# A hybrid decoder layer on one core: the decay tile in quarters, two longer waits, gate chunks moved to other buffers

## The chip, the core and the metric

The kernel runs on one core of one Trainium2 chip. The metric is device time in microseconds (us) of one execution, input in device memory to output in device memory. TensorE (PE) does matmuls, VectorE (DVE) and ScalarE (ACT) elementwise work, GpSimd (POOL) elementwise work and some transfers, SyncE (SP) only issues transfers. Each engine runs its instructions in the order in which the program lists them for it; it waits for another engine or for a transfer by semaphore, and everything behind a waiting instruction on that engine waits too.

## What is computed

One layer over a sequence of 1024 positions, model width 2048, float32, cut to what matters here:

```python
xn   = rms_norm(h, norm_w)
proj = xn @ w_in                                  # 2048 x 7184
qkv, z_a, b_raw, a_raw, u_b, v_b, z_b = split(proj)
q, k, v = split(silu(causal_conv4(qkv)))          # 8 heads x 128, q and k l2-normalised
beta = sigmoid(b_raw)
g    = -exp(a_log) * softplus(a_raw + dt_bias)    # log decay per head and position
gc   = cumsum(g)                                  # inside chunks of 64
decay = where(incl, exp(where(incl, gc[i] - gc[j], 0)), 0)
L    = where(strict, (k*beta) @ k.T * decay, 0)   # (I + L) solved per chunk
attn = where(incl, q @ k.T * decay, 0)
# state recurrence over chunks -> o_a ; o_a = rms_norm(o_a) * silu(z_a)
s    = chunked_causal_spatial(layer_norm(v_b))    # 128x128 matrix per group
o_b  = u_b * s * silu(z_b)
out  = rms_norm(h + concat(o_a, o_b) @ w_out)
```

## The kernel before

The sequence is done in two halves of 512 positions, one after the other (names end in 0 or 1 for the half: `em0`, `wl1_17_3`). A float32 product is done as three matmuls: each operand is split into a rounded part (`h`) and the rest (`l`), and PE does x_h w_h, x_l w_h and x_h w_l (L235, L236, L238). The splits of the weights are made on the spot: SP loads a raw chunk (`wr`, L184), ACT rounds it (`wh`, L134), DVE subtracts (`wl`, L135). A projection of 128 output columns has 48 matmuls in four chunks (`wl0_17_0` to `wl0_17_3` are the four chunks of column block 17 in half 0).

**Order.** `run` (L210) walks through the chunks, with the loads of the next ones started ahead. Work that belongs to a finished projection (convolution, gates, the solve of a pair of heads, output of a pair) is written as generators: `yield n` hands back for n ticks, and `tick` is called after every six matmuls or so of a projection. A scheduler then fixes each engine's order at build time. So a `yield` says how many matmuls stand between two steps in PE's order, and what stands between them in the order of the other engines follows.

**First tiles** (`first_tiles`, L259). Each half starts with one chunk loop over 16 blocks of the model width, which makes the first key and query projections (`wrf`, `whf`, `wlf`; banks 0 and 1) and, in four more PSUM banks, the 16 gate columns together with 256 columns of the spatial value (`V0` = 272 columns). The latter's chunks (`wrv0`, then `whv`, `wlv`) are called gate chunks below: eight of them, [128, 2, 272], in the same weight buffers as all others (tags `wr`, `wh`, `wl`), which are therefore 2176 bytes per partition long.

**Buffers of 8 KB** (pool `big`, tag `b8`, four of them). They hold, at various times, the keys and queries of a pair (`kq`), the spatial values (`vn`), the decay tile (`em`), a solve buffer (`fs`), and in the output phase the four blocks of output rows (`h`, stored at L829).

**Decay tile** (`task_gates`, L378 to L389). The cumulative log decay is written to device memory and read back broadcast into `em`, a tile of [128, 32 x 64]. Four times in a row: POOL subtracts (L386), DVE takes the minimum with a mask (L387), ACT takes the exponential (L388). `task_q` of each head waits until the whole tile is entered (L488), multiplies its own 4 x 64 columns on POOL (L491), and makes the products `gl` (L502) and `gae` (L509) on DVE.

**Pairs** (`task_pair`, L535). Inside the solve, PE fills `yp` (L572), ACT copies it negated to `ys` (L576), `yield 1`, and PE multiplies again (L581). At the end of a pair POOL scales the output `o` (L649), a transposed copy goes through device memory (`swap`, L410: DVE L415, POOL's transfers L420 and L423), and after `yield W_SWO` (L654, 16 ticks) DVE makes the gated result from the reloaded `ut` (L660), which SP stores.

**Spatial groups** (L728 to L737): PE fills `sp` (L732), DVE reads it into `s` (L734), POOL scales (L737). `s` shares two buffers (`ut`) with the reloaded tiles of the last pair, and `sp` shares two PSUM banks (tag `gen`) with other small products.

Of the kernel before, what the change touches and what calls it, by code (L numbers as in the profile page):

```python
# [8 lines left out]
F32 = mybir.dt.float32  # L9
F32R = mybir.dt.float32r  # L10
# [7 lines left out]
P = 128  # L18
# [5 lines left out]
NT = T // P  # L24
# [7 lines left out]
def kernel(ctx, tc, x_tok, x_t, w_in, w_v0, w_vb, w_out, conv_w, norm_w, a_log, dt_bias,  # L32
# [5 lines left out]
    wp = pool("wp", bufs=4)  # L38
    big = pool("big", bufs=4)
# [11 lines left out]
    def bc(ap, shape):  # L51
        return ap.broadcast_to(shape)
# [126 lines left out]
        nc.scalar.copy(rb, rp)  # L179
        return rb  # L180

    def w_chunk(src, shape, name, keep=None):
        raw = wp.tile(shape, F32, tag="wr", bufs=3, name=f"wr{name}")
        nc.sync.dma_start(raw, src)  # L184
        hi, lo = keep or (wp.tile(shape, F32R, tag="wh", name=f"wh{name}"), wp.tile(shape, F32R, tag="wl", name=f"wl{name}"))
        split(hi, lo, raw)
        return hi, lo
# [38 lines left out]
    V0 = 256 + 2 * H  # L226
# [32 lines left out]
    def first_tiles(hf, xs, env, done):  # L259


        accs, sqs = [], []
        for q in range(KT // 2):
            def prep(q=q):
                ks = slice(2 * q, 2 * q + 2)
                raw = wp.tile([P, 2, 2, P], F32, tag="wr", bufs=3, name=f"wrf{hf}_{q}")
                hi = wp.tile([P, 2, 2, P], F32R, tag="wh", name=f"whf{hf}_{q}")
                lo = wp.tile([P, 2, 2, P], F32R, tag="wl", name=f"wlf{hf}_{q}")
                sqs_, sqs[:] = list(sqs), []
                for i in range(2):  # L270
                    x, sq = x_load(hf, 2 * q + i)
                    xs.append(x)
                    sqs.append(sq)
                    nc.sync.dma_start(raw[:, i], w_in[(H, 0)[i], :, ks, :])
                    split(hi[:, i], lo[:, i], raw[:, i])
                vb = w_chunk(w_v0[q], [P, 2, V0], f"v0{hf}_{q}")
                for sq in sqs_ + (sqs if q == KT // 2 - 1 else []):
                    sq()
                if hf == 0 and q == 5:
                    conv_constants()  # L280
                return hi, lo, vb
# [32 lines left out]
    def task_gates(hf, accs, env, gt):  # L314
# [65 lines left out]
        em = big.tile([P, H * NT, 64], F32, tag="b8", name=f"em{hf}")  # L380
        for c in range(2):
            nc.gpsimd.dma_start(em[c * 64:(c + 1) * 64], gcd[c].partition_broadcast(64))
        yield 3
        for q in range(4):
            e4 = em[:, q * 8:(q + 1) * 8, :]
            nc.gpsimd.tensor_tensor(e4, e4, bc(gc[:, q * 8:(q + 1) * 8].unsqueeze(2), [P, 8, 64]), op=ALU.subtract)  # L386
            nc.vector.tensor_tensor(e4, e4, bc(cap.unsqueeze(1), [P, 8, 64]), op=ALU.min)  # L387
            nc.scalar.activation(e4, e4, AF.Exp)  # L388
        gt.update(em=em)  # L389


    def scaled(acc, rb, name):
# [39 lines left out]
        return s4  # L432


    W_SWO = 16
    W_SO0 = 4
    W_CONV = 7
    W_SWAP = 7
# [5 lines left out]
    W_DMA2 = 18  # L444
    W_GATES = 12
    W_LN = 12

    def task_k(hf, h, st, pr, acc):
        gt, hh = st["gt"], h % 2
# [29 lines left out]
    def task_q(hf, h, st, pr, acc):  # L479
        gt, hh = st["gt"], h % 2  # L480
        hd = pr["hd"][hh]
# [3 lines left out]
        yield W_SW0  # L485
        z = swap(y, kq[:, 1, :], y, f"q{hf}_{h}", nc.sync)
        yield W_CONV + (W_FIRST if h == 0 else 0)
        while "em" not in gt or "kd" not in hd:  # L488
            yield 1
        em = gt["em"][:, h * NT:(h + 1) * NT, :]  # L490
        nc.gpsimd.tensor_tensor(em, em, bc(hd["c"].unsqueeze(2), [P, NT, 64]), op=ALU.mult)  # L491

        wq = wk.tile([P, NT, 4, 64], F32, tag="wq", bufs=2, name=f"wq{hf}_{h}")
# [18 lines left out]
        if hh == 1:  # L512
            spawn(task_pair(hf, h // 2, st, pr))
# [23 lines left out]
    def task_pair(hf, p, st, pr):  # L537
        gt, heads = st["gt"], pr["hd"]
# [35 lines left out]
        for c in range(2):  # L574
            b = c * 64 + 32
            nc.scalar.activation(ys[b:b + 32], yp[b:b + 32], AF.Copy, scale=-1.0)  # L576
        yield 1
        for c in range(2):
            a, b = c * 64, c * 64 + 32
            for u in range(2 * NT):  # L580
# [52 lines left out]
        for h2, hd in enumerate(heads):  # L633
# [19 lines left out]
            yield 1  # L653
        yield W_SWO  # L654
        while not all("z" in hd for hd in heads):
# [298 lines left out]
```

## Time and profile before

| | us |
|---|---|
| median of 3 runs | 1827.82 (1825.97 to 1830.06) |
| the profiled execution, own time | 1829.9 |
| its span, first to last instruction | 1828.2 |
| PE busy | 1794.5 (98%) |
| DVE busy | 1149.2 (63%) |
| ACT busy | 733.1 (40%) |
| POOL busy | 263.0 (14%) |

The mean granted TensorE clock of the profiled execution is 0.992 of full speed. In a timeline row, the first column is the start, counted from the first instruction, the second the time from the start of the first to the end of the last of the instructions put together in the row; the count stands behind the x, and brackets give how long the engine had been idle before, with what released it. Matmuls overlap: one of 512 columns takes 0.4 us from start to end, but starts follow each other at 0.23 to 0.24 us. In the windows, PEclk is the mean granted TensorE clock of the stretch.

### The profile page before, as it was taken

Reading aid. Unit: us, or ns where it says so; the run is one execution under the profiler, and the core shown is the slowest. Engines: PE = TensorE matmul, PEld = TensorE weight load, DVE = VectorE, ACT = ScalarE, POOL = GpSimd, SP = SyncE. Lnnn points to the kernel's source line nnn. Section 1 sums busy time; section 2 is a strip of 40 time slices with the busy share of each in tenths; the row PEclk is TensorE's granted clock in tenths of the full one; section 3 lists DMA queues with packets and bytes.
Section 4 is the critical chain, followed back from the end, with each engine's and each line's share of the span. In section 5 each row is a group of like instructions: output and inputs, shape, how many; then the busy total and the mean of one; then the engine's idle time right before and its main releaser. Section 6 shows DMA issues by size and latency. Waiting matters only on the chain.

```text
span 1828.2 us, 27404 instructions
## 1 busy us (share of the span) xinstructions
PE 1794.5 (98%) x9526; PEld 1496.2 (82%) x9526; DVE 1149.2 (63%) x2797; ACT 733.1 (40%) x1656; POOL 263.0 (14%) x318
## 2 busy tenths in 40 slices
PE   9989999999999999999999899999999999999997
PEld 8878788888997888888888687887889978888886
DVE  7788697987646334433657887969785553344343
ACT  6543535445242222322636445354442422233232
POOL 3120130301202000011302101212021030000110
PEclk9999999999999999999999999999999999999999
DMA  7545354464424334733455453544544243355443
GB/s 223 134 130 139 90 143 123 112 164 117 134 81 138 103 103 129 219 121 116 132 194 145 119 139 96 155 107 123 140 122 129 78 122 101 100 158 158 123 140 132
DMA packets 164410, 239.16 MB, mean 131 GB/s; under 512 B 35472, under 2 KB 64176, under 8 KB 164016
## 3 DMA queue, kind: packets, MB, share of 16 engines
q1 hardware_dynamic: 154656, 215.35, 41.5%
q0 software_dynamic: 4864, 13.67, 3.0%
q10 hardware_dynamic: 4752, 8.40, 1.5%
q8 instruction: 74, 1.21, 0.3%
q14 instruction: 64, 0.52, 0.1%
HBM read 200.61 MB, written 36.73 MB: 130 GB/s over the span
## 4 chain that ended last, share of the span: by engine, by line
PE 88%; DVE 4%; DMA 4%; ACT 2%; issue 1%; SPq 0%; POOL 0%; ACTq 0%; POOLq 0%; DVEq 0%
PE acc L235 17%; PE acc L238 16%; PE acc L236 16%; PE vb L775 7%; PE oa L884 6%; PE oa L883 6%; PE oa L885 6%; PE ds L620 2%; PE p L609 1%; DMA wr<-w_in 1%; DVE cv L403 1%; PE ga L500 1%; PE up L594 1%; PE wp L599 1%; PE sp L732 1%
## 5 line engine op out<-in xcount | busy, mean ns | idle before, releaser
L235 PE MATMUL acc<-xh,wh 128*128 128x512 f32 x1472 | 599.3, 407 | 2.5 <-ACT wh L134 2.5
L238 PE MATMUL acc<-xh,wl 128*128 128x512 f32 x1472 | 584.7, 397 | 9.1 <-DVE wl L135 9.0
L236 PE MATMUL acc<-xl,wh 128*128 128x512 f32 x1472 | 580.7, 395 | 0.0
L134 ACT CAST wh<-wr 128x512 fp32r<-128x512 f32 x368 | 226.8, 618 | 493.6 <-PE acc L236 413.9
L135 DVE TENSOR_TENSOR wl<-wr,wh 128x512 fp32r<-128x512 f32 x368 | 255.6, 696 | 178.9 <-ACT wh L134 177.4
L238 PEld LDWEIGHTS acc<-xh,wl 128*128 128x128 f32 x1472 | 279.0, 190 | 75.2 <-DVE wl L135 10.7
L235 PEld LDWEIGHTS acc<-xh,wh 128*128 128x128 f32 x1472 | 278.7, 189 | 62.2 <-issue 3.5
L236 PEld LDWEIGHTS acc<-xl,wh 128*128 128x128 f32 x1472 | 279.3, 190 | 57.7 <-issue 0.7
L885 PE MATMUL oa<-who,ml 128*128 128x512 f32 x472 | 185.3, 393 | 0.0
L884 PE MATMUL oa<-wlo,mh 128*128 128x512 f32 x472 | 185.1, 392 | 0.0
L883 PE MATMUL oa<-who,mh 128*128 128x512 f32 x472 | 185.1, 392 | 0.0
L135 DVE TENSOR_TENSOR wlo<-wro,who 128x512 fp32r<-128x512 f32 x118 | 89.0, 756 | 145.6 <-ACT who L134 145.5
L134 ACT CAST who<-wro 128x512 fp32r<-128x512 f32 x118 | 72.7, 617 | 149.4 <-PE oa L885 140.1
L775 PE MATMUL vb<-whvb,xh 128*128 128x256 f32 x384 | 110.7, 288 | 0.0
L403 DVE SCALAR_TENSOR_TENSOR cv<-pc,cw,cv 128x511 f32<-128x511 f32 (+1 forms) x144 | 107.8, 749 | 4.6 <-ACT cv L400 2.6
L775 PE MATMUL vb<-whvb,xl 128*128 128x256 f32 x384 | 108.4, 282 | 0.0
L775 PE MATMUL vb<-wlvb,xh 128*128 128x256 f32 x384 | 108.3, 282 | 0.0
L884 PEld LDWEIGHTS oa<-wlo,mh 128*128 128x128 f32 x472 | 88.6, 188 | 20.3
L883 PEld LDWEIGHTS oa<-who,mh 128*128 128x128 f32 x472 | 88.6, 188 | 20.1
L885 PEld LDWEIGHTS oa<-who,ml 128*128 128x128 f32 x472 | 88.5, 188 | 20.0
L556 DVE TENSOR_TENSOR fs<-fs,fst 32x31 f32<-32x31 f32 (+15 forms) x248 | 88.5, 357 | 4.1
L554 DVE TENSOR_TENSOR fst<-fs 32x31 f32<-32x31 f32 (+15 forms) x248 | 87.3, 352 | 4.1
(239 smaller groups left out, 2366.4 us busy)
## 6 DMA issues: line engine op xcount, KB each, us to landing
wr<-w_in SPq DMA_DIRECT2D x368, 256.0 KB, 3.1
wro<-w_out SPq DMA_DIRECT2D x128, 256.0 KB, 2.7
wrvb<-w_vb SPq DMA_DIRECT2D x48, 256.0 KB, 2.7
xr<-x_t SPq DMA_DIRECT2D x32, 256.0 KB, 3.9
mr<-mix_d ACTq DMA_DIRECT2D x32, 256.0 KB, 3.4
xres<-x_tok SPq DMA_DIRECT2D x32, 256.0 KB, 3.5
out<-h SPq DMA_DIRECT2D x14, 512.0 KB, 2.8
wrv<-w_v SPq DMA_DIRECT2D x16, 272.0 KB, 2.8
```

The source lines that it names most:

```text
L134: nc.scalar.copy(hi, src)
L135: nc.vector.tensor_tensor(lo, src, hi.bitcast(F32), op=ALU.subtract)
L235: nc.tensor.matmul(acc, hi[:, kk, :], xh, start=(k == 0), stop=False)
L236: nc.tensor.matmul(acc, hi[:, kk, :], xl, start=False, stop=(last and lo is None))
L238: nc.tensor.matmul(acc, lo[:, kk, :], xh, start=False, stop=last)
L403: nc.vector.scalar_tensor_tensor(cv[:, s:], acc[:, :T - s], w, cv[:, s:], op0=ALU.mult, op1=ALU.add)
L554: nc.vector.tensor_tensor(tv, bc(lu[:, k, k + 1:].unsqueeze(2), [32, n, m]), bc(xu[:, k:k + 1, 0:m], [32, n, m]), op=ALU.mult)
L556: nc.vector.tensor_tensor(xu[:, k + 1:, 0:m], xu[:, k + 1:, 0:m], tv, op=ALU.subtract)
L775: nc.tensor.matmul(a, l[:, tsl], r[:, k % 2, :], start=fl, stop=sp_, skip_group_check=True)
L883: nc.tensor.matmul(acc[t], mh[:, tsl], hi[:, 0, :], start=(k == 0), stop=False)
L884: nc.tensor.matmul(acc[t], mh[:, tsl], lo[:, 0, :], start=False, stop=False)
L885: nc.tensor.matmul(acc[t], ml[:, tsl], hi[:, 0, :], start=False, stop=(k == k1))
```

## The change

Four things are changed. The gate chunks no longer use the weight buffers: the raw data of three chunks go into one 8 KB buffer (`v0r`), and each chunk's rounded part and rest together into another (`v0`), from the pool with tag `b8`. The weight buffers are then all 2048 bytes per partition. The decay tile is entered quarter by quarter: each quarter (two heads) is subtracted on POOL, then after two ticks minimum and exponential follow, and `task_q` of a head waits for its own quarter only; the wait before the first quarter is 5 ticks in place of 3. `W_SWO` is 20 in place of 16. The wait between the two `yp` products is 3 ticks in place of 1.

```diff
--- before.py
+++ after.py
@@ -179,8 +179,9 @@
         nc.scalar.copy(rb, rp)
         return rb
 
-    def w_chunk(src, shape, name, keep=None):
-        raw = wp.tile(shape, F32, tag="wr", bufs=3, name=f"wr{name}")
+    def w_chunk(src, shape, name, keep=None, raw=None):
+        if raw is None:
+            raw = wp.tile(shape, F32, tag="wr", bufs=3, name=f"wr{name}")
         nc.sync.dma_start(raw, src)
         hi, lo = keep or (wp.tile(shape, F32R, tag="wh", name=f"wh{name}"), wp.tile(shape, F32R, tag="wl", name=f"wl{name}"))
         split(hi, lo, raw)
@@ -259,7 +260,7 @@
     def first_tiles(hf, xs, env, done):
 
 
-        accs, sqs = [], []
+        accs, sqs, vraw = [], [], []
         for q in range(KT // 2):
             def prep(q=q):
                 ks = slice(2 * q, 2 * q + 2)
@@ -273,7 +274,10 @@
                     sqs.append(sq)
                     nc.sync.dma_start(raw[:, i], w_in[(H, 0)[i], :, ks, :])
                     split(hi[:, i], lo[:, i], raw[:, i])
-                vb = w_chunk(w_v0[q], [P, 2, V0], f"v0{hf}_{q}")
+                if q % 3 == 0:
+                    vraw.append(big.tile([P, 3, 2, 288], F32, tag="b8", name=f"v0r{hf}_{q}"))
+                v2 = big.tile([P, 2, 2, 288], F32R, tag="b8", name=f"v0{hf}_{q}")[:, :, :, 0:V0]
+                vb = w_chunk(w_v0[q], None, None, (v2[:, 0], v2[:, 1]), vraw[-1][:, q % 3, :, 0:V0])
                 for sq in sqs_ + (sqs if q == KT // 2 - 1 else []):
                     sq()
                 if hf == 0 and q == 5:
@@ -380,13 +384,16 @@
         em = big.tile([P, H * NT, 64], F32, tag="b8", name=f"em{hf}")
         for c in range(2):
             nc.gpsimd.dma_start(em[c * 64:(c + 1) * 64], gcd[c].partition_broadcast(64))
-        yield 3
+        yield W_EM
+
+        gt["em"] = []
         for q in range(4):
             e4 = em[:, q * 8:(q + 1) * 8, :]
             nc.gpsimd.tensor_tensor(e4, e4, bc(gc[:, q * 8:(q + 1) * 8].unsqueeze(2), [P, 8, 64]), op=ALU.subtract)
+            yield 2
             nc.vector.tensor_tensor(e4, e4, bc(cap.unsqueeze(1), [P, 8, 64]), op=ALU.min)
             nc.scalar.activation(e4, e4, AF.Exp)
-        gt.update(em=em)
+            gt["em"].append(e4)
 
 
     def scaled(acc, rb, name):
@@ -432,7 +439,7 @@
         return s4
 
 
-    W_SWO = 16
+    W_SWO = 20
     W_SO0 = 4
     W_CONV = 7
     W_SWAP = 7
@@ -444,6 +451,7 @@
     W_DMA2 = 18
     W_GATES = 12
     W_LN = 12
+    W_EM = 5
 
     def task_k(hf, h, st, pr, acc):
         gt, hh = st["gt"], h % 2
@@ -485,9 +493,9 @@
         yield W_SW0
         z = swap(y, kq[:, 1, :], y, f"q{hf}_{h}", nc.sync)
         yield W_CONV + (W_FIRST if h == 0 else 0)
-        while "em" not in gt or "kd" not in hd:
-            yield 1
-        em = gt["em"][:, h * NT:(h + 1) * NT, :]
+        while len(gt.get("em", ())) <= h // 2 or "kd" not in hd:
+            yield 1
+        em = gt["em"][h // 2][:, hh * NT:(hh + 1) * NT, :]
         nc.gpsimd.tensor_tensor(em, em, bc(hd["c"].unsqueeze(2), [P, NT, 64]), op=ALU.mult)
 
         wq = wk.tile([P, NT, 4, 64], F32, tag="wq", bufs=2, name=f"wq{hf}_{h}")
@@ -574,7 +582,7 @@
         for c in range(2):
             b = c * 64 + 32
             nc.scalar.activation(ys[b:b + 32], yp[b:b + 32], AF.Copy, scale=-1.0)
-        yield 1
+        yield 3
         for c in range(2):
             a, b = c * 64, c * 64 + 32
             for u in range(2 * NT):
```

The lines behind the change are eight higher in the new file at the places below (L387 is L394, L502 is L510; L135 stays).

DVE in half 0, from the minimum on the decay tile to the products of head 0, before. `em0` is the decay tile, `wl0_17_0` the rest of the first weight chunk of column block 17, `gl0_0` and `gae0_0` head 0's products:

```order
L130 SCALAR_TENSOR_TENSOR ce0_1_1098<-rst_k0_1_1100,ce0_1_1098 128x4
L387 TENSOR_TENSOR em0_972<-em0_972,cap_96 128x512 x4
L467 TENSOR_TENSOR nk0_1_1096<-ce0_1_1098,ssk0_1_1090 128x4
L468 TENSOR_TENSOR cc0_1_1097<-ce0_1_1098 128x4
L135 TENSOR_TENSOR wl0_17_0_1124<-wr0_17_0_1121,wh0_17_0_1123 128x512
L502 TENSOR_TENSOR gl0_0_1070<-ga0_0_1061,em0_972 128x256
L509 TENSOR_TENSOR gae0_0_1073<-ga0_0_1061,em0_972 64x4x64 x2
```

and now, from the first minimum on:

```order
L394 TENSOR_TENSOR em0_959<-em0_959,cap_96 128x512
L484 TENSOR_TENSOR kd0_1_1068<-pc0_9_864,ce0_1_1048 128x512
L135 TENSOR_TENSOR wl0_17_0_1074<-wr0_17_0_1071,wh0_17_0_1073 128x512
L422 STREAM_TRANSPOSE pc0_1_1011<-kq0_0_756 128x4x4x32
L135 TENSOR_TENSOR wl0_17_1_1105<-wr0_17_1_1102,wh0_17_1_1104 128x512
L394 TENSOR_TENSOR em0_959<-em0_959,cap_96 128x512
L510 TENSOR_TENSOR gl0_0_1123<-ga0_0_1114,em0_959 128x256
L517 TENSOR_TENSOR gae0_0_1126<-ga0_0_1114,em0_959 64x4x64 x2
L135 TENSOR_TENSOR wl0_17_2_1149<-wr0_17_2_1146,wh0_17_2_1148 128x512
L401 TENSOR_TENSOR pc0_16_1164<-acc0_16_1026,rb0_713 128x512
L394 TENSOR_TENSOR em0_959<-em0_959,cap_96 128x512
L415 COPY tails_126<-pc0_16_1164 128x3
```

The four minima stood together ahead of `wl0_17_0`. Now one stands ahead of it, together with head 1's scaled key `kd0_1`, and the other three stand between the chunks that follow.

DVE in half 1, the rows up to the rest of the last chunk of column block 17 (`wl1_17_3`), before; the four minima and `gl1_0` stand further ahead:

```order
L469 TENSOR_TENSOR cc1_1_9788<-cc1_1_9788,g1_beta_9419 128x4
L405 SCALAR_TENSOR_TENSOR cv1_16_9875<-tails_126,cw_99,cv1_16_9875 128x2
L470 TENSOR_TENSOR ce1_1_9789<-cc1_1_9788,g1_ekd_9622 128x4
L403 SCALAR_TENSOR_TENSOR cv1_16_9875<-pc1_16_9873,cw_99,cv1_16_9875 128x509
L476 TENSOR_TENSOR kd1_1_9809<-pc1_9_9564,ce1_1_9789 128x512
L405 SCALAR_TENSOR_TENSOR cv1_16_9875<-tails_126,cw_99,cv1_16_9875 128x3
L135 TENSOR_TENSOR wl1_17_3_9887<-wr1_17_3_9884,wh1_17_3_9886 128x512
```

and now (`cv1_16` is the convolution of column block 16, `pc1_16` its input):

```order
L484 TENSOR_TENSOR kd1_1_9746<-pc1_9_9538,ce1_1_9726 128x512
L394 TENSOR_TENSOR em1_9635<-em1_9635,cap_96 128x512
L410 SCALAR_TENSOR_TENSOR cv1_16_9844<-pc1_16_9842,cw_99,cv1_16_9844 128x511
L412 SCALAR_TENSOR_TENSOR cv1_16_9844<-tails_126,cw_99,cv1_16_9844 128x1
L410 SCALAR_TENSOR_TENSOR cv1_16_9844<-pc1_16_9842,cw_99,cv1_16_9844 128x510
L510 TENSOR_TENSOR gl1_0_9801<-ga1_0_9792,em1_9635 128x256
L517 TENSOR_TENSOR gae1_0_9804<-ga1_0_9792,em1_9635 64x4x64 x2
L412 SCALAR_TENSOR_TENSOR cv1_16_9844<-tails_126,cw_99,cv1_16_9844 128x2
L410 SCALAR_TENSOR_TENSOR cv1_16_9844<-pc1_16_9842,cw_99,cv1_16_9844 128x509
L412 SCALAR_TENSOR_TENSOR cv1_16_9844<-tails_126,cw_99,cv1_16_9844 128x3
L394 TENSOR_TENSOR em1_9635<-em1_9635,cap_96 128x512
L135 TENSOR_TENSOR wl1_17_3_9859<-wr1_17_3_9856,wh1_17_3_9858 128x512
```

Here `wl1_17_3` still stands behind the convolution, head 0's products and three of the four minima; the fourth is behind it. `kd1_1` has moved in front of the convolution.

PE at the start of half 1, rows of the first block, before (`first1_0` and `first1_1` are the key and query banks, `first1_2` to `first1_5` those of the gate chunks):

```order
L294 MATMUL first1_1_8891<-xh1_0_8714,whf1_0_8710 128x512
L295 MATMUL first1_1_8891<-xl1_0_8715,whf1_0_8710 128x512
L296 MATMUL first1_1_8891<-xh1_0_8714,wlf1_0_8711 128x512
L299 MATMUL first1_2_8892<-whv01_0_8732,xh1_0_8714 128x272
L300 MATMUL first1_2_8892<-wlv01_0_8733,xh1_0_8714 128x272
L301 MATMUL first1_2_8892<-whv01_0_8732,xl1_0_8715 128x272
```

and now, where the first gate chunk (`v01_0`) is used:

```order
L300 MATMUL first1_1_8872<-xh1_10_9038,wlf1_5_9035 128x512
L298 MATMUL first1_0_8871<-xh1_11_9047,whf1_5_9034 128x512
L299 MATMUL first1_0_8871<-xl1_11_9048,whf1_5_9034 128x512
L300 MATMUL first1_0_8871<-xh1_11_9047,wlf1_5_9035 128x512
L298 MATMUL first1_1_8872<-xh1_11_9047,whf1_5_9034 128x512
L303 MATMUL first1_2_8873<-v01_0_8718,xh1_0_8701 128x272
L303 MATMUL first1_3_8874<-v01_0_8718,xh1_0_8701 128x272
L303 MATMUL first1_4_8875<-v01_0_8718,xh1_0_8701 128x272
```

The first use of a gate chunk was the seventh matmul of the half. It is now the 71st, behind those of blocks 0 to 10 and most of block 11 for key and query; the matmuls of the gate chunks follow after that. On SP, the first three gate loads of half 1 now stand behind the stores of the first two blocks of output rows of half 0, the next three behind those of all four.

## Rows read from the trace of the kernel before

**Rows 1.** The page: busy time, share of the span and instructions of each engine

```profile
PE 1794.5 (98%) x9526; PEld 1496.2 (82%) x9526; DVE 1149.2 (63%) x2797; ACT 733.1 (40%) x1656; POOL 263.0 (14%) x318
```

**Rows 2.** Timeline of PE: start, us, engine, line, tiles [idle before <-releaser]

```profile
97.25 0.80 PE L238 MATMUL acc<-xh,wl 128*128 128x512 f32 x1 [5.92 <-DVE wl L135]
...
186.74 1.07 PE L581 MATMUL yp<-tt,ys 32*32 32x32 f32 x32 [1.74 <-ACT ys L576]
...
579.54 1.47 PE L732 MATMUL sp<-wmt,vn 128*128 128x128 f32 x8 [2.06 <-DVE s L734]
...
1009.61 0.50 PE L235 MATMUL acc<-xh,wh 128*128 128x512 f32 x1 [2.48 <-ACT wh L134]
...
1013.45 0.79 PE L238 MATMUL acc<-xh,wl 128*128 128x512 f32 x1 [3.11 <-DVE wl L135]
...
1201.19 0.97 PE L581 MATMUL yp<-tt,ys 32*32 32x32 f32 x28 [0.87 <-ACT ys L576]
...
1485.15 0.80 PE L732 MATMUL sp<-wmt,vn 128*128 128x128 f32 x2 [2.74 <-DVE s L734]
```

**Rows 3.** Windows: start:end, length, busy of each engine, PEclk, DMA share, GB/s

```profile
96.00:102.00 6.00, 4.75 (x11) 3.79 (x12) 5.92 (x15) 2.51 (x5) 1.11 (x2) 0.50 0.44 109
188.00:192.00 4.00, 4.00 (x17) 3.42 (x18) 2.75 (x14) 0.75 (x2) 0.00 (x0) 0.61 0.46 112
580.00:584.00 4.00, 4.00 (x16) 3.34 (x15) 3.42 (x4) 0.00 (x0) 1.80 (x3) 0.57 0.53 179
1013.00:1018.00 5.00, 4.55 (x12) 3.62 (x13) 3.95 (x9) 2.05 (x4) 0.00 (x0) 0.59 0.63 165
1199.00:1207.00 8.00, 7.13 (x66) 5.80 (x65) 5.06 (x19) 3.97 (x13) 1.04 (x1) 1.00 0.37 90
```

**Rows 4.** Timeline of DVE, half 0, at the decay tile

```profile
90.60 5.42 DVE L387 TENSOR_TENSOR em<-em,cap 128x512 f32<-128x512 f32 x4 [2.44 <-POOL em L386]
...
96.51 0.68 DVE L135 TENSOR_TENSOR wl<-wr,wh 128x512 fp32r<-128x512 f32 x1
```

**Rows 5.** Timeline of POOL, the decay subtracts of both halves

```profile
89.52 4.94 POOL L386 TENSOR_TENSOR em<-em,gs 128x512 f32<-128x512 f32 x4 [4.80 <-DMA em<-gcd]
...
998.29 4.58 POOL L386 TENSOR_TENSOR em<-em,gs 128x512 f32<-128x512 f32 x4 [2.25 <-DMA em<-gcd]
```

**Rows 6.** Timeline of DVE, half 1, at the decay tile

```profile
999.28 0.69 DVE L135 TENSOR_TENSOR wl<-wr,wh 128x512 fp32r<-128x512 f32 x1 [3.79 <-ACT wh L134]
...
999.89 1.01 DVE L465 TENSOR_SCALAR ssk<-ssk 128x4 f32<-128x4 f32 x1
...
1004.70 2.49 DVE L387 TENSOR_TENSOR em<-em,cap 128x512 f32<-128x512 f32 x4
...
1008.43 0.42 DVE L502 TENSOR_TENSOR gl<-ga,em 128x256 f32<-128x256 f32 x1 [0.51 <-POOL em L491]
...
1012.71 1.28 DVE L135 TENSOR_TENSOR wl<-wr,wh 128x512 fp32r<-128x512 f32 x2
```

**Rows 7.** Timeline of POOL, half 0, last pair, transfers of the two heads

```profile
564.50 2.99 POOL L420 DMA_DIRECT2D swapo<-ut  x4 [1.04 <-DVE ut L415]
...
573.62 0.57 POOL L423 DMA_DIRECT2D ut<-swapo  x1
```

**Rows 8.** Timeline of DVE, half 0, last pair

```profile
577.94 0.75 DVE L660 SCALAR_TENSOR_TENSOR o<-ut,hnw,z 128x512 f32<-128x512 f32 x1 [2.55 <-DMA ut<-swapo]
```

**Rows 9.** Timeline of PE, first matmuls of half 1

```profile
912.81 0.40 PE L294 MATMUL first<-xh,whf 128*128 128x512 f32 x1
913.05 0.40 PE L295 MATMUL first<-xl,whf 128*128 128x512 f32 x1
```

**Rows 10.** Timeline of SP, the output stores of half 0

```profile
920.30 9.15 SPq L829 DMA_DIRECT2D out<-h  x8
```

**Rows 11.** The page, DMA issues: out<-in, engine, count, KB each, us to landing

```profile
out<-h SPq DMA_DIRECT2D x14, 512.0 KB, 2.8
```

**Rows 12.** Timeline of DVE, last normalisation of an output row block

```profile
927.66 0.74 DVE L824 SCALAR_TENSOR_TENSOR h<-h,sth,fw 128x512 f32<-128x512 f32 x1
```

## The prediction

> **What bounds the kernel now.** I read the page's table of busy times first. PE is busy 1794.5 us [rows 1] of a span of 1828.2 us, the profiled execution's own time being 1829.9 us. So no matmul goes away and at most some 33 us can be won: the places where PE stands, and the slow clock after them. Then I went through PE's timeline for idle time in brackets. Seven stalls matter [rows 2]: 5.92 us in half 0 and 2.48 and 3.11 us in half 1 where a weight split is late (released by DVE's `wl` or ACT's `wh`), 1.74 and 0.87 us before the second `yp` product (released by ACT's copy `ys`), 2.06 and 2.74 us before a spatial product (released by DVE's `s`). Sum: 18.92 us. The rest of PE's idle time is in gaps of under half a microsecond, the first microsecond and the output chain behind the last matmul; the change does not touch these.
>
> The third view is the windows behind the stalls. There the granted clock is near the lower of its two levels (1.2 of 2.4 GHz) [rows 3], and what that costs is the busy time multiplied by what is missing from 1: 4.75 x 0.50 = 2.4 us after the 5.92-us stall, 4.00 x 0.39 = 1.6 after the 1.74, 4.00 x 0.43 = 1.7 after the 2.06, 4.55 x 0.41 = 1.9 after the two of half 1; for the 2.74 I put 1.7 as an estimate from the 2.06. After the 0.87 the clock is 1.00: that one costs only itself. Together 9.3 us. All that the change can take away at these seven places is therefore 28.2 us.
>
> **Decay tile, half 0.** PE wanted `wl0_17_0` at 97.25 - 5.92 = 91.33 us [rows 2]. On DVE it stood behind four minima of 5.42 us in all, which began at 90.60 when POOL's first quarter was there, and two small instructions; it ran from 96.51 for 0.68 us [rows 4]. Now one minimum and `kd0_1` stand ahead of it. The four minima lay beside POOL's four subtracts (4.94 us from 89.52 [rows 5]) and took 5.42 / 4 = 1.36 us each; the four of half 1, after POOL had finished at 1002.87, took 2.49 / 4 = 0.62 [rows 5, 6]. So I take 1.36 for the one minimum, and 0.68 (the row of `wl`) for `kd0_1` and `wl0_17_0` each: 90.60 + 1.36 + 0.68 + 0.68 = 93.3. The stall is then 2.0 us, with 1.7 us of slow clock behind it, as after the 2.06: 3.7 in place of 8.3, a gain of 4.6 us. If nothing is slowed by POOL, the split ends at 92.6, the stall is 1.3, and the clock may hold as it did after 0.87: a gain of 7.0. If all three are slowed to 1.36, it ends at 94.7: stall 3.3 and 1.9 of clock, a gain of 3.1. The later minima and chunks alternate, some 2.8 us (twelve matmuls) apart, which covers one minimum and one split even at 1.36 each.
>
> Is `wl` slowed by POOL? In half 1 a `wl` ran 0.69 us from 999.28, inside POOL's stretch of subtracts (998.29 to 1002.87), not slower than alone; the instruction of four columns behind it took 1.01 [rows 5, 6]. The Trainium skill (GPSIMD Engine Reference, Specifications) has POOL share its SBUF interfaces with VectorE and names contention for DVE instructions with two SBUF inputs, which speaks against this change, since `kd0_1` and `wl0_17_0` now run among the subtracts. By the rule the gain here is the 3.1 of the last bound, by the row 4.6. The minima bear the rule out and this `wl` does not.
>
> **Decay tile, half 1.** PE wanted the last chunk of block 17 at 1009.61 - 2.48 = 1007.13, first its rounded part, then the rest [rows 2]. ACT now has the rounded part ahead of the exponentials and the convolution, so the 2.48 goes. The rest, `wl1_17_3`, began at 1012.71 [rows 6] and ended about 1013.4. It still stands on DVE behind a long row. From the first minimum: three minima 1.9, `kd1_1` 0.7, three convolution steps at 0.75 = 2.3 (the price of the same kind in [rows 8]), `gl` and two `gae` at 0.42 = 1.3, the split itself 0.7, some four small ones at 0.2 (half of `gl`) = 0.8, and the wait of 0.5 before `gl` for POOL: 8.2 us. The minima began at 1004.70. DVE stood idle for 3.79 us before 999.28 because `wl1_17_2` came first; five steps of the inverse square root are now in front of it and can fill that. Against this, four small steps are now ahead of the minima. I take 2.0 us earlier: 1002.7 + 8.2 = 1010.9 and, since PE needs the rest only two matmuls after the first, a stall of about 3.4. That is 2.2 less than 5.59, with the clock lost as before: a gain of 2.2. Bounds: none if the chain starts no earlier (a stall of 5.4), 3.8 if all the idle time is filled; a full cure, 7.5, is the far end.
>
> **The `yp` wait.** From 1 to 3 ticks puts eighteen matmuls instead of six between the two products: 12 x 0.23 = 2.8 us [rows 9], more than the 1.74 by which ACT was late. Both stalls and the 1.6 of clock go: 4.2 us. The next products of these pairs come 2.8 us later and PE has projections in between, so nothing is late behind them; if that cover failed in each of eight pairs at the 0.87 of the smaller stall, 7 us would be lost, which I hold for unlikely and leave to the range.
>
> **The output wait, 16 to 20 ticks.** It is the last pair of each half that counts. DVE waited 2.55 us for the reload of the first head's `ut`, and `s`, which uses the same buffers, stood behind the gated output L660 of 0.75 us at 577.94 [rows 8]; PE's stall of 2.06 followed. The first head's stores were issued from 564.50 to 567.49, but its reload only at 573.62, behind the second head's first store on POOL [rows 7]. In the new order the reload follows its own stores directly. It may be 6.1 us earlier, and the product that all this starts from is twelve matmuls (2.8 us) later: 3.3 us net, against a stall of 2.06. But the second head's product, in one of the two small banks, now waits for the first `s`, and L660 comes four ticks (5.6 us) later in the order. I leave 1.0 us of stall in each half, with no loss of clock: (2.06 + 1.7 - 1.0) + (2.74 + 1.7 - 1.0) = 6.2 us. Bounds: 0 (the wait moves) and 8.2.
>
> **Gate chunks.** The number and size of loads and splits stay, so in half 0, where the four 8 KB buffers are free, I put 0. In half 1 all four hold output rows. PE begins at 912.81 and reaches the first gate chunk 70 matmuls later, 70 x 0.235 = 16.4 us [rows 9]: 929.2. SP's eight stores went out from 920.30 over 9.15 us [rows 10]; the first four by 924.9, and the three loads behind them land, at a store's 2.8 us [rows 11], at about 927.7; splitting the first adds 0.7 on ACT and DVE each: 929.1. That is even with the need. The third chunk's buffer is the last block's, normalised at 928.4 [rows 12], stored about 932; the next three raw loads wait for it. I put 1.5 us. Bounds: 0; and 8.5 for one complete wait (first split only at 936, a stall of 6.8 with 1.7 of clock).
>
> **Sum.** 4.6 + 2.2 + 4.2 + 6.2 - 1.5 = 15.7 us, from 1829.9: 1814.2. The median of the runs shown is 2.1 us below the profiled execution, so that runs may lie at 1812 to 1814. I say 1814.
>
> **Rivals.**
> - All seven stalls go. For it: each is one instruction too late, not an engine at its limit (DVE 63%, [rows 1]). Against: in half 1 the order itself keeps three minima and the convolution in front. 1829.9 - 28.2 = 1801.7.
> - The decay tile's stall is only half mended and the spatial stall moves: 3.1 (POOL slows all three DVE steps to 1.36) + 0 + 4.2 + 3.0 - 1.5 = 8.8, which gives 1821. (Its first term is the case that the Trainium skill's GPSIMD Engine Reference, Specifications, speaks for.) For it: the rows in front of `wl1_17_3`, and two buffers for `s` and `ut` as before. Against: `wh` is no longer behind the exponentials.
> - Slower: gate chunks wait for the output stores. The mechanism is SP's order: the raw loads stand behind the stores of blocks that DVE finishes only at 928.4, and each group of three waits for a buffer that the group before holds. One wait costs 8.5 us; two cost 17, which is what the other parts win (17.2), and three give 1829.9 - 17.2 + 25.5 = 1838. From two full waits on it decides the sign. For it: no slack at the first chunk in my own sum. Against: 70 matmuls of cover ahead and twelve more for each later pair of blocks.
>
> **How the numbers follow.** The forecast has 0.55, with its own range 1808 to 1820; all stalls gone 0.13; half mended 0.18; late gate chunks 0.14, of which 0.06 end near no change and 0.08 slower. A measurement of this kernel can tell about 0.2%, 3.7 us, from no change. Faster: 0.55 + 0.13 + 0.18 = 0.86, less 0.01 for the half-mended case's upper tail. The range leaves out half of the first rival and most of the last: 1804 to 1826.
>
> **What would show it.** In the new trace: `wl0_17_0` ending at 93 to 94 us and PE's stall there near 2 us; in half 1 no stall on a `wh`, but one of about 3 on `wl1_17_3`; no gap before the second `yp` product; a gap of at most 1 us around the last pair; at the start of half 1 the first gate chunk's split within a microsecond of PE's need. I am wrong if a stall of over 5 us stands at the gate chunks, or if PE waits in half 1 at the decay tile for nothing.

## The result and the profile after

The changed kernel takes 1802.98 us (median of 4 runs, 1801.94 to 1806.62) beside 1827.45 us of the kernel before (4 runs, 1825.97 to 1830.06): a ratio of 0.9868 (0.985 to 0.9886), so it is 1.3% faster. The forecast was 1814 with a range from 1804. The direction is right, the gain is 24.5 us in place of 15.7, and the time lies just under the range. It is close to the 1801.7 us of the rival in which all stalls go, but not for its reason: PE stands longer than before.

The page of the changed kernel has this for the engines:

```profile
PE 1762.8 (98%) x9526; PEld 1491.1 (83%) x9526; DVE 1148.0 (64%) x2797; ACT 732.6 (41%) x1658; POOL 262.6 (15%) x318
```

The span is 1800.7 us (1828.2 before), so PE's idle time (span less busy time) went up from 33.7 to 37.9 us, and its busy time went down by 31.7 us with the same 9526 instructions [rows 1]. The whole gain is in matmuls that take less time, which the prediction had excluded.

Part of it is the clock. In windows of the changed kernel that answer to those of before [rows 3] (and one over the start of half 1):

```profile
96.00:102.00 6.00, 6.00 (x39) 4.71 (x38) 5.92 (x12) 2.78 (x5) 0.00 (x0) 1.00 0.86 204
188.00:192.00 4.00, 4.00 (x20) 3.69 (x20) 0.69 (x1) 1.39 (x5) 1.04 (x1) 0.67 0.28 80
900.00:950.00 50.00, 50.00 (x309) 45.09 (x308) 28.64 (x92) 22.73 (x49) 1.29 (x1) 1.00 0.54 181
```

The stretch after the decay tile of half 0 has the full clock now (it was 0.50); after the first pair's solve it is 0.67 (it was 0.61). PE has no idle time at all from 900 to 950 us, where the gate chunks of half 1 are first used.

The larger part shows where nothing stalls and the clock is full. In the output phase of half 0, the same 150 us in the kernel before and in the changed one (the number behind PE's busy time counts its instructions):

```profile
740.00:890.00 150.00, 150.00 (x653) 122.28 (x652) 61.96 (x91) 53.14 (x99) 21.70 (x17) 1.00 0.48 148
```

```profile
740.00:890.00 150.00, 150.00 (x664) 124.19 (x663) 65.65 (x97) 59.38 (x109) 25.95 (x21) 1.00 0.44 131
```

653 instructions before, 664 now: one start every 229.7 ns and every 225.9 ns. Over the whole program I added up what the 512-column matmuls, apart from those before a stall or another product, take from start to start beyond 227 ns: at full clock 39.5 us before and 18.6 now, at the low clock 10.9 and 5.7. So of the 31.7 us, 20.9 are closer starts at full clock and 5.2 the clock; the rest, 5.6, is left for the other matmuls. The sums depend on how strictly those exceptions are left out, but the first difference stays at 21 to 22 us however it is done. Matmuls of 256 columns gained nothing: they start 121.4 ns apart before and 121.7 now (in all such means, starts over 300 ns apart are left out).

The stalls that remain, in PE's timeline of the changed kernel (compare [rows 2]):

```profile
82.01 0.50 PE L236 MATMUL acc<-xh,wh 128*128 128x512 f32 x1 [1.20 <-ACT wh L134]
...
83.73 0.50 PE L239 MATMUL acc<-xh,wl 128*128 128x512 f32 x1 [0.99 <-DVE wl L135]
...
94.86 0.50 PE L239 MATMUL acc<-xh,wl 128*128 128x512 f32 x1 [1.42 <-DVE wl L135]
...
186.88 1.74 PE L602 MATMUL up<-bv,tt 128*128 128x128 f32 x8 [2.88 <-DVE tt L593]
...
996.00 0.79 PE L239 MATMUL acc<-xh,wl 128*128 128x512 f32 x1 [6.18 <-DVE wl L135]
...
1188.95 1.13 PE L602 MATMUL up<-bv,tt 128*128 128x128 f32 x8 [2.66 <-DVE tt L593]
```

Half 0's decay tile waits 1.42 us in place of 5.92, but two new waits of 1.20 and 0.99 us stand ahead of it. Half 1 waits 6.18 us in place of 2.48 and 3.11. The waits before `yp` are gone, and waits before the next product, `up`, have come. Grouped by line, with the idle time in the last column:

```profile
L602 PE MATMUL up<-bv,tt 128*128 128x128 f32 x128 | 17.9, 284 | 11.7 <-DVE tt L593 11.7
...
L740 PE MATMUL sp<-wmt,vn 128*128 128x128 f32 x128 | 17.0, 276 | 0.6 <-DVE o L646 0.6
```

11.7 us before `up`, where there was none; before `sp` 0.6 in place of 4.8.

### The profile page after: what moved, and what is told of

Its sections match the earlier page's. It is cut to its first block, busy times and chain, and to the rows that moved or that the text cites. A ratio compares the mean times of both kernels' runs of the same rounds, so it can differ in the third digit from the quotient of the medians.

```text
span 1800.7 us, 27391 instructions
## 1 busy us (share of the span) xinstructions
PE 1762.8 (98%) x9526; PEld 1491.1 (83%) x9526; DVE 1148.0 (64%) x2797; ACT 732.6 (41%) x1658; POOL 262.6 (15%) x318
## 4 chain that ended last, share of the span: by engine, by line
PE 75%; DVE 13%; DMA 6%; ACT 3%; issue 3%; SPq 1%; POOL 0%; ACTq 0%; DVEq 0%; POOLq 0%
PE acc L236 12%; PE acc L239 12%; PE acc L237 12%; PE vb L783 8%; PE oa L891 6%; PE oa L893 6%; PE oa L892 6%; DVE wl L135 3%; DMA wr<-w_in 2%; DVE cv L410 2%; PE p L617 1%; PE ds L628 1%; DMA pc<-swapk 1%; DVE fs L564 1%; DVE fst L562 1%
## 5 line engine op out<-in xcount | busy, mean ns | idle before, releaser
L236 PE MATMUL acc<-xh,wh 128*128 128x512 f32 x1472 | 591.3, 402 | 1.2 <-ACT wh L134 1.2
L239 PE MATMUL acc<-xh,wl 128*128 128x512 f32 x1472 | 576.4, 392 | 8.6 <-DVE wl L135 8.6
L135 DVE TENSOR_TENSOR wl<-wr,wh 128x512 fp32r<-128x512 f32 x368 | 253.5, 691 | 161.5 <-ACT wh L134 160.1
L135 DVE TENSOR_TENSOR wlo<-wro,who 128x512 fp32r<-128x512 f32 x118 | 88.8, 754 | 142.6 <-ACT who L134 142.5
L892 PEld LDWEIGHTS oa<-wlo,mh 128*128 128x128 f32 x472 | 88.6, 188 | 18.3
L562 DVE TENSOR_TENSOR fst<-fs 32x31 f32<-32x31 f32 (+15 forms) x248 | 91.9, 371 | 4.5
L564 DVE TENSOR_TENSOR fs<-fs,fst 32x31 f32<-32x31 f32 (+15 forms) x248 | 84.8, 342 | 4.0
```

The costliest lines, as they stand in the source:

```text
L135: nc.vector.tensor_tensor(lo, src, hi.bitcast(F32), op=ALU.subtract)
L236: nc.tensor.matmul(acc, hi[:, kk, :], xh, start=(k == 0), stop=False)
L239: nc.tensor.matmul(acc, lo[:, kk, :], xh, start=False, stop=last)
L562: nc.vector.tensor_tensor(tv, bc(lu[:, k, k + 1:].unsqueeze(2), [32, n, m]), bc(xu[:, k:k + 1, 0:m], [32, n, m]), op=ALU.mult)
L564: nc.vector.tensor_tensor(xu[:, k + 1:, 0:m], xu[:, k + 1:, 0:m], tv, op=ALU.subtract)
L892: nc.tensor.matmul(acc[t], mh[:, tsl], lo[:, 0, :], start=False, stop=False)
```

## The experiments

Each run is compared with runs of the kernel before on the same chip; times are medians. The kernel before took 1825.19 to 1827.99 us in these comparisons, so a difference of 2 to 3 us between runs on different chips shows nothing by itself.

**Where the weight buffers lie.** A matmul reads two operands here, the activations and a split weight. The compiled programs tell where they lie: the activations start at 64 modulo 256 bytes in both kernels. With the three raw buffers ahead of them and 2176 bytes each, the split weights start in turn at 192, 64, 192, 64 modulo 256; with 2048 bytes, all at 64. So a theory (address theory): starts are slow where the two operands of a matmul lie differently modulo 256. The rival (stall theory): the gain is in the stalls and the clock. Four kernels tell them apart.

`pad2304`, the order of before and longer buffers:

```diff
+    # wh, wl: [P, 576] allocated and the first part used; wr as before
+    wp.tile([P, 32], F32, name="gap", tag="gap", bufs=1)
```

> The kernel before with one edit: the eight buffers for the rounded part and the rest of the weights (wh, wl) are 2304 bytes per partition in place of 2176 and start 128 bytes further on, so that all of them have the same start address modulo 256 as the activations (64), as they have in the changed kernel. The order of the instructions is that of before. Address theory (the gain comes from matmul starts that follow each other at 227 ns in place of 231, because of where the weight buffers lie): 5952 matmuls at 3.8 ns less, about 1805 us, and the seven stalls of before stay as they are. Stall theory (the gain is the stalls and the slow clock behind them, as predicted): no change, 1827 us.

Measured 1812.28 us, ratio 0.9914 (0.9896 to 0.9932). Its 150 us:

```profile
740.00:890.00 150.00, 150.00 (x663) 124.25 (x662) 64.17 (x95) 56.03 (x103) 23.93 (x20) 1.00 0.47 144
```

663 instructions, as good as the changed kernel, with every engine's order as before. Of the some 22 us that closer starts give, some are lost again: idle time in PE's gaps (without the time behind its last matmul) grows from 24.3 to 29.5 us. I read this as the stalls of before meeting a PE that is earlier, but this profile is of the slowest of the four runs (1819.0 us), and its first long stall is shorter than before (4.75 us in place of 5.92).

`pad2176`, the changed kernel with the old length (`wp.tile([P, 544], ...)`, the first part used):

> The changed kernel with one edit: its weight buffers are 2176 bytes long again, with nothing in the last 128 bytes. Address theory: starts of matmuls at about 231 ns again, 1824 to 1827 us. Stall theory: it stays at 1803 us.

Measured 1812.29 us, 0.9919 (0.9904 to 0.9933): 9.3 us of the gain gone.

```profile
740.00:890.00 150.00, 150.00 (x653) 122.27 (x652) 63.72 (x94) 57.42 (x105) 24.69 (x20) 1.00 0.43 132
```

`sched`, the scheduling parts without the gate chunks' move:

```diff
-                vb = w_chunk(w_v0[q], None, None, (v2[:, 0], v2[:, 1]), vraw[-1][:, q % 3, :, 0:V0])
+                vb = w_chunk(w_v0[q], [P, 2, V0], f"v0{hf}_{q}")
```

> The kernel before with the decay tile in quarters and the two longer waits, but the gate chunks still in the weight buffers (2176 bytes). Stall theory, by the prediction's terms without its 1.5 us for the gate chunks: 1810 to 1812 us. Address theory: the idle time is about that of the changed kernel, which had more of it (28.6 us in all) than before (24.3), less by what its slow clock costs less; 1822 to 1829 us.

Measured 1814.29 us, 0.9931 (0.9913 to 0.9949), between the two: better than the address theory allowed. Its starts are those of before:

```profile
740.00:890.00 150.00, 150.00 (x653) 122.27 (x652) 64.77 (x96) 56.92 (x105) 23.07 (x19) 1.00 0.45 136
```

`gate`, only the gate chunks' move (`yield W_EM` and the quarters, 20 and `yield 3` undone):

> The kernel before with the gate chunks moved out of the weight buffers (2048 bytes), the decay tile and both waits as before. Address theory: nearly the whole gain, 1802 to 1808 us. Stall theory: 1827 to 1829 us, since by the prediction this part alone costs 1.5 us.

Measured 1812.14 us, 0.9916 (0.989 to 0.9942).

```profile
740.00:890.00 150.00, 150.00 (x663) 124.28 (x662) 66.04 (x98) 58.49 (x107) 24.67 (x20) 1.00 0.45 135
```

So both are at work: 13.7 us from the scheduling parts, 15.8 from the move (11 to 20 by its interval); together 24.5 in place of 29.5. The two padded kernels say the same of the move: the addresses are worth 15.7 us with the order of before and 9.3 with the new one. The stalls tell where the rest went: 18.3 and 19.0 us of gaps in PE's timeline in `pad2176` and `sched`, 28.6 in the changed kernel. That a faster PE reaches the same late steps earlier is my reading of this; no run isolates it.

Next, what it is in the address. `shiftw128` puts a gap between activations and weights, `shift128` the same gap ahead of both:

```diff
+    wp.tile([P, 32], F32, name="gap", tag="gap", bufs=1)    # shiftw128; shift128: cst.tile
```

> The changed kernel with 128 unused bytes between the activations and the weight buffers: every weight buffer starts at 192 modulo 256, the activations stay at 64. In the kernel before half of the weight buffers lay so, and matmul starts cost 22 us more. Both address theories (what counts is the distance between the two operands; or: what counts is where the weights lie) say slow matmuls, 231 ns or more, 1812 us if half of them being off is as bad as all, up to 1835 us if the loss doubles. Theory that only unequal spacing of the buffers costs: no change, 1803 us.

Measured 1819.14 us, 0.9966 (0.9953 to 0.9978).

```profile
740.00:890.00 150.00, 150.00 (x648) 121.57 (x647) 63.00 (x94) 56.62 (x104) 24.74 (x20) 1.00 0.43 130
```

> The changed kernel with 128 unused bytes ahead of both activations and weight buffers: both start at 192 modulo 256. If the distance between the two operands counts: no change, 1803 us, matmul starts 227 ns apart. If the place of the weights counts: slow as with the weights alone moved, 1812 us or more.

Measured 1801.88 us, 0.9873 (0.985 to 0.9896).

```profile
740.00:890.00 150.00, 150.00 (x664) 124.24 (x663) 66.17 (x98) 59.28 (x109) 25.58 (x21) 1.00 0.45 132
```

648 against 664. For shifts by 128 bytes it is the distance between the two operands that counts, not the place of either. `shiftw64` makes it 64 bytes (`wp.tile([P, 16], ...)`):

> The changed kernel with 64 unused bytes between the activations and the weight buffers: the operands are 64 bytes apart modulo 256, where 0 gave 227 ns between matmul starts and 128 gave 232. If only the half of 256 counts that an address lies in, or if 64 is a step on the way: some slow starts, 1805 to 1815 us. If any distance but 0 costs as much as 128: 1819 us. If 64 costs nothing: 1803 us.

Measured 1814.24 us, 0.9921 (0.9901 to 0.9941).

```profile
740.00:890.00 150.00, 150.00 (x657) 123.19 (x656) 64.75 (x96) 57.90 (x106) 24.80 (x20) 1.00 0.44 130
```

657 instructions in this stretch, less slow than at 128; over the whole program 46.6 us beyond 227 ns against 49.1, nearly as much. The loss is uneven at 64: starts inside the projections (`acc`) are 233.3 ns apart, those in the output phase 228.9, and there one start in three follows after 225.9. Both have fewer microseconds of stalls (12.4 and 14.8, the changed kernel 28.6).

**The waits.** `no_y` sets the wait between the `yp` products back to 1, `y33` adds one behind it:

```diff
-        yield 3        # no_y: before the second yp product
+        yield 1
-        yield 1        # y33: before up
+        yield 3
```

> The changed kernel with the wait between the two yp products back at 1 tick. The prediction's term (the longer wait gains 4.2 us): 1807 us. Theory that the longer wait only moves the stall (in the changed kernel PE waits 2.88, 0.86, 1.27, 2.47, 2.66 and 1.56 us, 11.7 us in all, for the copy of yp into tt before the next product): the stalls go back to the ys copy, with some 3 to 8 us in all, so 1796 to 1803 us.

Measured 1807.34 us, 0.9897 (0.988 to 0.9914); the longer wait gains 4.4 us by the medians, 6.6 if each kernel is taken against the kernel before on its chip.

```profile
L740 PE MATMUL sp<-wmt,vn 128*128 128x128 f32 x128 | 18.4, 291 | 5.6 <-DVE s L742 5.6
...
L589 PE MATMUL yp<-tt,ys 32*32 32x32 f32 x256 | 8.8, 193 | 3.7 <-ACT ys L584 3.6
```

The `yp` waits are back, and with them 5.6 us before `sp`, while those before `up` are gone.

> The changed kernel with the next wait of the pair, between the copies of yp into tt and the product up, at 3 ticks in place of 1. If the stalls before up are only a matter of six matmuls of cover: the 11.7 us of stalls and some 4 us of slow clock behind the longer ones go, 1788 to 1792 us. If DVE is behind with everything there: the stall shows at the next product, 1800 to 1803 us.

Measured 1800.21 us, 0.986 (0.9844 to 0.9876). The wait before `up` falls to 0.1 us, but others come: 5.1 us before `ds`, 2.5 before `wp`, 1.7 before `yp`.

`no_swo` sets the output wait back (`W_SWO = 16`), `sched_swo16` does the same to `sched`:

> The changed kernel with the output wait back at 16 ticks. By the prediction's term (6.2 us, the stalls before the spatial product): 1809 us. Rival: the kernel with only the yp wait undone had those stalls back (2.31 and 3.33 us) although the wait was 20, so the order that removes them does not hang on this wait: 1803 us.

Measured 1795.06 us, 0.9821 (0.9805 to 0.9838), less than the changed kernel.

```profile
L602 PE MATMUL up<-bv,tt 128*128 128x128 f32 x128 | 18.0, 286 | 5.8 <-DVE tt L593 5.8
```

> The kernel before with the decay tile in quarters and the yp wait at 3 ticks, but the output wait at 16 and the gate chunks in the weight buffers of 2176 bytes. In PE's order the products of the last pair and the spatial groups stand as in the changed kernel. If the yp wait alone has taken the stalls before the spatial product away: about the 1814 us of the kernel that has all three of these parts, or up to 8 us less, since the longer output wait cost 8 us beside short weight buffers. If the output wait does it: the stalls of 2.06 and 2.74 us are back, 1820 us.

Measured 1815.18 us, 0.9938 (0.9923 to 0.9952); with the wait at 20 it was 1814.29.

```profile
L598 PE MATMUL up<-bv,tt 128*128 128x128 f32 x128 | 17.9, 285 | 2.5 <-DVE tt L589 2.5
...
L736 PE MATMUL sp<-wmt,vn 128*128 128x128 f32 x128 | 17.1, 276 | 0.6 <-DVE o L642 0.6
```

No stall before `sp` that is worth naming at 16 ticks either, with the old buffers. The longer output wait does not cure it; the `yp` wait does. To see whether the 8 us are the wait's, both kernels ran again on one chip.

> The changed kernel itself, on one chip with the run beside it. 1802 to 1804 us if what was measured for it holds on this chip.

> The changed kernel with the output wait at 16, unchanged from the run that took 1795 us. If the 8 us come from the output wait: 1794 to 1796 us, 8 us below its neighbour, with fewer microseconds of stalls before up. If the earlier difference was one between chips or sittings: the same as its neighbour within 2 us.

Measured 1802.78 us, 0.9862 (0.9844 to 0.988), and 1798.75 us, 0.9847 (0.983 to 0.9864). The difference is 4.0 us here, with overlapping intervals; the stalls before `up` are 9.9 us with 20 ticks and 6.1 with 16 (11.7 and 5.8 in the first runs). In this second profile of the changed kernel one wait before the second `yp` product is back, with 1.62 us, so 3 ticks only just cover it. So 16 is not worse beside the short buffers, and 4 to 8 us better by the medians. How this wait reaches `up` is open.

**The decay tile.** `no_em` enters it whole again:

> The changed kernel with the decay tile entered whole again, as before. By the prediction's terms (4.6 us in half 0, 2.2 in half 1): 1810 us. Rival: the changed kernel still waits 6.18 us for wl1_17_3, more than the 5.59 of before, so half 1 gained nothing, and only half 0's term is lost: 1807 us.

Measured 1806.02 us, 0.9881 (0.9867 to 0.9896).

```profile
98.03 0.79 PE L239 MATMUL acc<-xh,wl 128*128 128x512 f32 x1 [5.89 <-DVE wl L135]
...
1002.20 0.79 PE L239 MATMUL acc<-xh,wl 128*128 128x512 f32 x1 [7.04 <-DVE wl L135]
```

The quarters are worth 3.0 us by the medians, with overlapping intervals: 4.5 of stall at `wl0_17_0` in half 0, little in half 1 (7.04 against 6.18). The waits of 1.20 and 0.99 us ahead of it in half 0 are not there in `no_em`, so they are a cost of the quarters, and half 0's stalls fall by 2.3 us in all. `y33_em9` is `y33` with 9 ticks before the first quarter:

```diff
-    W_EM = 5
+    W_EM = 9
```

> The changed kernel with the wait before up at 3 ticks in place of 1 (as in the last experiment on it, 1800 us) and the wait before the first quarter of the decay tile at 9 ticks in place of 5. In DVE's order wl1_17_3 then stands ahead of all four minima of half 1. If the minima and what follows them are what makes it late: the 6.46 us stall and some 2 us of slow clock behind it go, about 1792 us. If it waits for its load or for the chain of small steps beside POOL's subtracts: 1797 to 1800 us.

Measured 1797.12 us, 0.9835 (0.982 to 0.9849). On DVE, and then on PE:

```profile
986.13 0.69 DVE L135 TENSOR_TENSOR wl<-wr,wh 128x512 fp32r<-128x512 f32 x1
...
986.81 0.69 DVE L394 TENSOR_TENSOR em<-em,cap 128x512 f32<-128x512 f32 x1
...
993.41 0.68 DVE L135 TENSOR_TENSOR wl<-wr,wh 128x512 fp32r<-128x512 f32 x1
```

```profile
994.15 0.66 PE L239 MATMUL acc<-xh,wl 128*128 128x512 f32 x1 [4.01 <-DVE wl L135]
```

The split at 986.13 is `wl1_17_3`, ahead of the first minimum and in time. PE now waits 4.01 us for the next chunk's, at 993.41: over a third of the 6.46 us of `y33` is gone and the rest has moved one chunk on.

> The changed kernel with the output wait at 16 and the wait before the decay tile's first quarter at 9. If the two gains add (8 us from the output wait; some 3 from wl1_17_3, which stood 5.77 us late with 5 ticks and 4.01 with 9): 1791 to 1793 us. If the later quarters only move the stall: 1795 us.

> As the run before, and the wait before up at 3 ticks. If the remaining stalls before up (2.00, 0.57, 0.68, 1.19, 1.06 us with the output wait at 16) are only cover: 1786 to 1790 us. If they move to the next products, as they did with the output wait at 20: 1791 to 1794 us.

Measured 1799.01 us, 0.9853 (0.9839 to 0.9868), and 1799.67 us, 0.985 (0.9833 to 0.9866). The gains do not add: in the first, PE waits 8.4 us before `up`, 2.6 more than with the output wait alone; in the second, 2.6 us before a split in half 0. The lowest median is that of the changed kernel with the output wait at 16 (1795 us, 1799 when run again); `y33_em9` with 1797 cannot be told from it.

## Why the prediction was wrong, step by step

**The step that failed** is the one on the gate chunks: "the number and size of loads and splits stay, so in half 0 ... I put 0", and 1.5 us of cost in half 1. The move made the weight buffers shorter, and with that every split weight came to lie like the activations modulo 256. Alone it is worth 15.8 us, and 11.3 beside the scheduling parts (1814.29 less 1802.98), of the other sign. The premise ahead of it failed too, that only stalls and the clock behind them can be won: the matmuls themselves were not at their pace. It could be seen in the trace of before, though not in a single pair of starts like that of [rows 9], 0.24 us apart: in its output phase the mean pace goes up and down from chunk to chunk, 228 ns and 232.6 ns. The feared wait for output stores did not come: PE ran without a pause from 900 to 950 us; a gate chunk cost 0.75 us in half 0 instead. (In the last two versions tried a gate chunk of half 1 was late, by 0.45 and 0.99 us.)

**Decay tile, half 0** was right in kind. DVE in the changed kernel:

```profile
88.10 1.05 DVE L130 SCALAR_TENSOR_TENSOR ce<-rst_k,ce 128x4 f32<-128x4 f32 x1
...
90.08 0.15 DVE L476 TENSOR_TENSOR cc<-ce 128x4 f32<-128x4 f32 x1
90.26 0.90 DVE L477 TENSOR_TENSOR cc<-cc,g_beta 128x4 f32<-128x4 f32 x1
91.19 0.97 DVE L478 TENSOR_TENSOR ce<-cc,g_ekd 128x4 f32<-128x4 f32 x1
...
92.09 0.68 DVE L394 TENSOR_TENSOR em<-em,cap 128x512 f32<-128x512 f32 x1
...
92.69 1.09 DVE L484 TENSOR_TENSOR kd<-pc,ce 128x512 f32<-128x512 f32 x1
...
93.70 1.09 DVE L135 TENSOR_TENSOR wl<-wr,wh 128x512 fp32r<-128x512 f32 x1
```

The minimum took 0.68, not 1.36, but began at 92.09 and not at 90.60, because four of the five small steps beside POOL's subtracts (88.09 to 92.14 us) took 0.90 to 1.05 us each (0.16 without POOL). `kd0_1` and `wl0_17_0` (93.70), beside POOL's next instructions, took 1.09 each, between my two prices of 0.68 and 1.36. The Trainium skill (GPSIMD Engine Reference, Specifications) names contention between POOL and DVE instructions with two SBUF inputs. These rows agree with it, except that the fifth small step, which reads one tile twice, took 0.15. The split ended at 94.8 (forecast 93.3, at most 94.7); the stall was 1.42 (2.0), as PE was later, held up by 1.20 and 0.99 before. My sum had no term for these two waits, which came with the quarters. No slow clock followed.

**Decay tile, half 1** was wrong: a gain of 2.2 forecast, none found (6.18 against 5.59; against `no_em`, 0.9). DVE there:

```profile
983.09 0.79 DVE L135 TENSOR_TENSOR wl<-wr,wh 128x512 fp32r<-128x512 f32 x1 [3.79 <-ACT wh L134]
...
988.67 0.68 DVE L394 TENSOR_TENSOR em<-em,cap 128x512 f32<-128x512 f32 x1
...
992.51 0.42 DVE L510 TENSOR_TENSOR gl<-ga,em 128x256 f32<-128x256 f32 x1 [0.50 <-POOL em L499]
...
995.26 0.68 DVE L135 TENSOR_TENSOR wl<-wr,wh 128x512 fp32r<-128x512 f32 x1
```

The length was right: from the first minimum at 988.67 to the end of the split at 995.94 is 7.3 us, forecast 8.2, with the forecast wait before `gl`. But `wl1_17_2` again kept DVE idle for 3.79 us, and the steps put ahead of it did not bring the minima forward against PE: PE wanted the rest at 996.00 - 6.18 = 989.82, 1.15 us after the first minimum began. Before, it was 2.9 us (1007.13 and two matmuls, less 1004.70).

**The `yp` wait** has its 4.2 us (4.4 measured), but by another sum. The stalls did go in the first profile, and the statement that nothing is late behind them was wrong. DVE before one of the `up` products:

```profile
1184.31 0.72 DVE L422 STREAM_TRANSPOSE pc<-kq 128x512 f32<-128x512 f32 x1 [3.26 <-ACT kq L492]
...
1187.88 0.40 DVE L593 COPY tt<-yp 32x256 f32<-32x256 f32 x1
...
1188.39 0.42 DVE L593 COPY tt<-yp 32x256 f32<-32x256 f32 x1
```

PE's second `yp` product in this pair was done about 1184.7; the copies of it into `tt` start only at 1187.88 and 1188.39, behind a transpose, before which DVE had stood idle for 3.26 us until ACT's `kq` was there, and behind the small steps of another head's inverse square root. `up` has six matmuls of cover. 11.7 us came in. What helped to pay for them is in PE's order around the last pair. Before, the second head's output product (`at`) stood between the first two spatial groups; in the changed kernel it stands behind both:

```profile
561.67 1.05 PE L732 MATMUL sp<-wmt,vn 128*128 128x128 f32 x8
...
563.95 1.06 PE L637 MATMUL at<-ut,gae 128*128 128x128 f32 x8
...
566.01 1.06 PE L732 MATMUL sp<-wmt,vn 128*128 128x128 f32 x8
```

```profile
554.41 1.05 PE L740 MATMUL sp<-wmt,vn 128*128 128x128 f32 x8
...
556.68 1.05 PE L740 MATMUL sp<-wmt,vn 128*128 128x128 f32 x8
...
571.47 1.13 PE L645 MATMUL at<-ut,gae 128*128 128x128 f32 x8 [0.35 <-DVE s L742]
```

The new order stands in `no_swo` and `sched_swo16` too, the old one in `no_y`: it comes with the `yp` wait and not with the output wait, and with it the 4.8 us before `sp` go.

**The output wait** was put at 6.2 us and is worth nothing with the old buffers (1814.29 and 1815.18 us), and a loss of 4 to 8 us with the short ones. The effect that I ascribed to it belongs to the `yp` wait.

Sum of the scheduling parts: 17.2 forecast, 13.7 measured with the old buffers. That this comes near is in part luck, since two of the four terms gave nothing and the stalls before the spatial product went by another cause.

## What to carry to other kernels

Before counting stalls, divide stretches without stalls at full clock by their matmuls, chunk by chunk: four nanoseconds per start were worth 21 us here, nearly as much as all gaps in PE's timeline (24.3 us), and the two paces of 228 and 232.6 ns could be seen before any change. When a change alters the length of a buffer, work out where all later buffers start, and compare the operands of each matmul modulo 256. A wait put in front of one late step is worth what is left when the next late step is counted. With faster matmuls the gaps added up to more in each pair of kernels here (24.3 to 25.2 and 29.5 us with the old order, 18.3 and 19.0 to 28.6 with the new one), and the two gains did not add.

## What was not expected of the hardware

A float32 matmul of 512 columns with its own weight load starts every 226 to 227 ns at full clock if its operands' start addresses agree modulo 256, and about 232 ns after the last, over the whole program, if they lie 64 or 128 bytes apart (at 64 between 226 and 233.5 on average, by which matmul follows which); a common shift of both by 128 bytes changes nothing, and buffers that alternate between 64 and 320 modulo 512 (`pad2304`) cost nothing. The output phase of the kernel before shows it chunk by chunk: 228 ns with the chunks whose buffers agree with the activations, 232.6 with the others. Matmuls of 256 columns show no loss: 121.4 ns before, 121.7 in the changed kernel, 121.1 at a distance of 128, 119.7 at 64. Which part of the memory or of the engine it comes from, and other distances, were not tried.
